# Joints between the stages of a one-layer encoder step: sums moved to VectorE, a kept pool, later norm and bias work, another product order

## The chip, the core and the metric

The kernel runs on one core of a Trainium2 chip. The metric is the device time of one execution in microseconds; the time of a version is the median of its runs. Times inside an execution come from one profiled execution.

## The reference

One inference step of a layer with d_model 2048 over 592 rows (512 prompt frames, 64 sample frames, 16 meta tokens), all in fp32:

```python
h = rmsnorm(x, g_mix)
u, q, k, v = split(h @ w_in)            # 1024 columns each
a = pool_scale * ((trailing_means(u) - u) @ w_pool)      # windows 2, 4, 8, 16
b = (1 - lambda_init) * subln(softmax(q1 k1 + bias) v - lam * softmax(q2 k2 + bias) v)  # 8 heads
x = x + concat(a, b) @ w_out
h = rmsnorm(x, g_ffn)
x = x + (silu(h @ w_gate) * (h @ w_up)) @ w_down         # d_ff 5632
y = rmsnorm(x, g_final)
```

The bias is a relative-position bias, looked up by a one-hot product. The outputs are y and the new rows of the caches and of the pooling state.

## The kernel before

**Precision.** Each fp32 operand is split into a high part (rounded to fp32r, a copy on ScalarE) and a low part (the difference, on VectorE), and each product is three matmuls: high times high, high times low, low times high (`mm3`, L112 to L114; in the class `Seven`, L796 to L798). So every weight tile costs ScalarE one copy and VectorE one subtraction (L137 and L138 with a gain per row, L132 and L133 without, L824 and L825 in the FFN, L994 and L995 in the down projection). Weights are loaded by SyncE's queue into raw tiles, and split from there.

**Order.** The program is written in stages, and a scheduler of the tile framework orders the instructions of each engine by the program's order, by the waits that it knows and by the buffers of the pools. Each engine executes its own list strictly in order; waits between engines are semaphores. What stands in a list behind a waiting instruction waits too.

**Head, to about 54 us.** x is loaded in pieces, transposed on TensorE (L201) and split (L106 on ScalarE, L107 on VectorE) into 16 tiles; `behind` holds the two instructions of the last split. K's first projection runs between the transposes as x and weights arrive; a projection has two halves of the columns, each in a PSUM bank of the pool `pj` (three banks). The rows of the relative-position bias are made by two small matmuls (L243) into two of these banks, copied to `t8` (L244), written to DRAM (`brow`, L247) and from there replicated to 128 partitions in DRAM (`brep`, L248, 3.1 MB), both through GpSimd's queue. Each head loads its piece of it (`bias`, L348) before its scores (L423).

**Heads and pooling projections, to about 583 us.** Eight heads of K, Q, V projections with attention between; then `proj_u(m)` for m = 0 to 7 (evacuation L545). Behind m = 1 come three splits of the attention's outputs (`split_head`), the 16 residual sums of x's high and low part into `hp` (L579, GpSimd), and m = 2 to 7.

**Out-projection, to about 810 us.** `out_proj(m, k0)` for 16 m, first with the second half of the inner dimension while the pooled mean and its map (evacuations L649, L650) run beside, then with the first half (k0 = 0). Between these the weights' pool `wts` is closed and opened anew as `wts2`; the squares of rows 4 to 15 are summed (L692 on ScalarE, L693 on GpSimd) into `accp`. `pre_scale` behind the second of the later out-projections multiplies accp by a matrix of 1/d (L701) for a first estimate of the norm. As the rows are finished, their squares go into `acc` (L755, L757), and `combine` forms the sums of operands that the FFN needs.

**FFN, 810 to 1809 us.** Gate and up are computed by a scheme of seven products per 2x2 block (Strassen and Winograd), for 22 f each. `Seven.prep(i)` makes the weights of product i: 0 is raw "11", 1 a combination of "11", "21" and "22" (L781 to L783), 2 an intermediate, 3 and 5 from "12" and the others (L785), 4 and 6 raw. `product(i)` issues the matmuls, and uses banks 0, 1, 2, 0, 1, 2, 1 for i = 0 to 6, each a running sum; `evac` moves out what stands in the bank before it is used again. `run` issues the products in order and prepares the weights three products ahead. Ahead of the first product `ffn_rstd` multiplies acc (L709) for the exact norm, and three further sets of operands are split (`xput`, L726 and L727).

**Down, 1809 to 2375 us.** 40 blocks (5 rounds x 8 m) of 2 to 5 pairs, 24 of them with 5 pairs, each seven products of 3 matmuls per pair with 288 columns. The operands are loaded from DRAM (`sx`), and split into `hc` (three per pair, for products 0 and 1, 2 and 3, 4 and 5) and `hh` (product 6), L981 and L982. Evacuations of products 1, 2, 4 and 5 are adds on VectorE into y (L1012), the others are copies on ScalarE and accumulating DMAs. The raw weights come into a ring of five buffers (L775), four loads a block. Two memsets (L1022, L1023) and a use of the Sqrt table (L1060) prepare the final norm; the latter is written in a hook behind the first block. The final norm and the output rows follow, to 2397 us.

The parts that the change touches most directly:

```python
for k in range(KT):
    nc.gpsimd.tensor_tensor(hrow(k), xs[k].bitcast(F32)[:, 0, NM:NT], xs[k].bitcast(F32)[:, 1, NM:NT], op=ALU.add)
bank, first = ((0, True), (1, True), (2, True), (0, False), (1, False), (2, False), (1, False))[i]
rw.tile([P, DJ, P], F32, name="raw", tag="raw", bufs=5)
```

Of the kernel before, what the change touches and what calls it, by code (L numbers as in the profile page):

```python
# [19 lines left out]
P = 128  # L20
# [3 lines left out]
NM = 16  # L24
# [26 lines left out]
def hymba_step(  # L51
# [23 lines left out]
    wts_stack = ExitStack()  # L75
# [87 lines left out]
    with tc.tile_pool(name="xraw", bufs=1, side="right") as xp, \  # L163
# [77 lines left out]
        for c0, c1 in ((0, 392), (392, RELW)):  # L241
            ps = pj.tile([P, 512], F32, name="pj")
            nc.tensor.matmul(ps[:HEADS, :c1 - c0], lhsT=tb, rhs=oh[:, c0:c1], start=True, stop=True)  # L243
            nc.vector.tensor_copy(t8[:, c0:c1], ps[:HEADS, :c1 - c0])  # L244
# [333 lines left out]
    for k in range(KT):  # L578
        nc.gpsimd.tensor_tensor(hrow(k), xs[k].bitcast(F32)[:, 0, NM:NT], xs[k].bitcast(F32)[:, 1, NM:NT], op=ALU.add)  # L579
    for m in range(2, HEADS):  # L580
        proj_u(m)
    for h in range(MXB, HEADS):
        split_head(h)
# [81 lines left out]
    wts_stack.close()  # L665
# [9 lines left out]
    wts = ffb.enter_context(tc.tile_pool(name="wts2", bufs=3, reuse_waits="tile"))  # L675
# [10 lines left out]
    for m in range(4, KT):  # L686
        hm = hrow(m)
        if m == 4:
            nc.scalar.activation(accp, hm, AF.Square)
            continue  # L690
        sq = xslot([P, NQ], "sqp")
        nc.scalar.activation(sq, hm, AF.Square)  # L692
        nc.gpsimd.tensor_tensor(accp, accp, sq, op=ALU.add)  # L693
# [67 lines left out]
    class Seven:  # L761


        def __init__(self, src, j0, nj, c0, raws, tmp, splits, xs_, psum, evac):
            self.src = src.rearrange("(j two p) n -> p two j n", p=P, two=2)[:, :, j0:j0 + nj, c0:c0 + 2 * P]
            self.nj, self.raws, self.tmp, self.splits, self.xs_, self.psum, self.evac = nj, raws, tmp, splits, xs_, psum, evac
            self.w, self.a = {}, None
# [21 lines left out]
        def product(self, i):  # L789
            if i == 0:  # L790
                self.b = self.psum()
# [9 lines left out]
    def run(seq, hooks=None, ahead=3):  # L801
        steps = [(n, i) for n in range(len(seq)) for i in range(7)]
        done = 0
        for pos, (n, i) in enumerate(steps):
            while done < len(steps) and done <= pos + ahead:
                dn, di = steps[done]
                seq[dn].load()
                seq[dn].prep(di)
                if di == 2 and dn + 1 < len(seq):
                    seq[dn + 1].load()  # L810
                done += 1
            seq[n].product(i)
            if hooks is not None:
                hooks(n, i)
# [57 lines left out]
    def gate_evac(f):  # L872
        def evac(s, i):
            if i == 0:
# [38 lines left out]
    for i in range(2):  # L913
        seq[0].prep(i)
    ffn_rstd()
    for p, blk in ((3, 2), (5, 3), (6, 1)):
# [4 lines left out]
    prep0 = seq[0].prep  # L921
    seq[0].prep = lambda i: None if i < 2 else prep0(i)
    run(seq)
    ffb.close()
    ffa.close()
    ffr.close()

# [25 lines left out]
    rw.tile([P, DJ, P], F32, name="raw", tag="raw", bufs=5)  # L953
# [11 lines left out]
    def h_free(f, q, n, i):  # L965
# [4 lines left out]
        return k < 0 or (last_use[k // 3], 2 * (k % 3) + 1) <= (n, i)  # L970
# [13 lines left out]
    def hooks(n, i):  # L984
        if queue and h_free(*queue[0], n, i):
            h_operand(*queue.pop(0))
        for f, q in queue:
            assert first_use[f] > n or (first_use[f] == n and 2 * q > i), (f, q, n, i)
# [33 lines left out]
    nc.vector.memset(stat, 1.0)  # L1022
    nc.vector.memset(eps, EPS)  # L1023
# [34 lines left out]
    def finished(n, i):  # L1058
        if n == 0 and i == 6:
# [5 lines left out]
    for n, (m, j0, j1) in enumerate(turns):  # L1065
        psum = (lambda: banks(pz, "mm", "mm")) if n % 2 == 0 else (lambda: banks(pj, "pj", "pj"))
        seq.append(Seven(w_down[0], j0, j1 - j0, m * 2 * P,
                         lambda n, nj=j1 - j0: rw.tile([P, DJ, P], F32, name="raw", tag="raw", bufs=5)[:, :nj],
# [9 lines left out]
    run(seq, hooks)  # L1078
# [60 lines left out]
```

## Time and profile before

| | |
|---|---|
| median of 3 runs | 2395.32 us (2386.61 to 2406.23) |
| the profiled execution | 2398.76 us, span 2396.9 us |
| busy in the span | TensorE 2277.7 us (95%), VectorE 1878.6 (78%), ScalarE 1143.0 (48%), GpSimd 553.7 (23%) |
| matmuls | 16815 |
| chain that ended last | TensorE 79%, DMA 8%, VectorE 7%, ScalarE 2%, GpSimd 1% |
| raw weights of the down projection | 112 loads of 320 KB, 4.5 us from issue to landing |

A busy time is the sum of the instructions' spans on an engine, not the time at its peak: a matmul at the low clock is as busy as one at the high. The chain follows back from the last instruction to what released it, and so shows where the time passed; the list of waits tells what an engine stood idle for, and names the releaser that came last. DMA issues stand as SPq or POOLq, the queues of SyncE and GpSimd.

### The profile page before, as it was taken

How to read it: one execution, taken by the hardware profiler on the slowest of the kernel's cores; microseconds unless marked ns; L12 is line 12 of the kernel's file. 1: busy time of each engine (PE TensorE's matmuls, PEld its weight loads, DVE VectorE, ACT ScalarE, POOL GpSimd, SP SyncE). 2: the span in 40 equal slices, each digit the busy share in tenths (PEclk: the TensorE clock that was granted, in tenths of full speed). 3: DMA queues.
4: the chain of work that ended last, by engine and by line, in shares of the span. 5: the costliest groups of instructions: out<-in, count | busy, mean ns of one | idle time of the engine just before them, and what ended most of it. 6: DMA issues, size and time to landing. Idle time of an engine off the chain costs nothing.

```text
span 2396.9 us, 43624 instructions
## 1 busy us (share of the span) xinstructions
PE 2277.7 (95%) x16815; PEld 2245.9 (94%) x16815; DVE 1878.6 (78%) x3445; ACT 1143.0 (48%) x2423; POOL 553.7 (23%) x483
## 2 busy tenths in 40 slices
PE   7999999979989899999999999999997999999995
PEld 6999999979989899999999999999996999999995
DVE  5888888765557788888888888888886777777786
ACT  5666666633234444444444444444445544444443
POOL 1000000041354322322322322332331022111121
PEclk9999999999989899999999999999998999999998
DMA  7333332223224243333333433433425478766643
GB/s 208 104 88 87 87 97 84 72 62 91 77 65 131 74 132 115 114 124 120 120 116 120 132 108 113 132 114 106 140 89 172 135 184 187 182 158 161 157 101 113
DMA packets 425875, 286.01 MB, mean 119 GB/s; under 512 B 12963, under 2 KB 405341, under 8 KB 425540
## 3 DMA queue, kind: packets, MB, share of 16 engines
q1 hardware_dynamic: 403184, 226.50, 32.9%
q0 software_dynamic: 21648, 55.30, 9.0%
q8 instruction: 132, 2.16, 0.4%
q10 hardware_dynamic: 836, 1.43, 0.2%
q14 instruction: 75, 0.61, 0.1%
HBM read 233.65 MB, written 40.35 MB: 114 GB/s over the span
## 4 chain that ended last, share of the span: by engine, by line
PE 79%; DMA 8%; DVE 7%; issue 3%; ACT 2%; POOL 1%; POOLq 0%; SPq 0%; DVEq 0%; ACTq 0%
PE mm L796 8%; PE pj L796 8%; PE mm L798 8%; PE mm L797 8%; PE pj L798 8%; PE pj L797 8%; PE pj L112 6%; PE pj L113 6%; PE pj L114 6%; DMA raw<-in_w_down_dram 4%; PE mm L114 3%; PE mm L112 3%; PE mm L113 3%; DVE ws L995 2%; DMA sx<-hd 1%
## 5 line engine op out<-in xcount | busy, mean ns | idle before, releaser
L825 DVE TENSOR_TENSOR ws<-raw,ws 128x512 fp32r<-128x512 f32 x430 | 384.5, 910 | 75.0 <-ACT ws L824 72.2
L824 ACT ACTIVATE ws<-raw 128x512 fp32r<-128x512 f32 x430 | 264.5, 630 | 347.5 <-PE pj L798 124.3
L796 PE MATMUL mm<-xc,ws 128*128 128x288 f32 x1232 | 365.4, 297 | 4.5 <-ACT ws L824 4.5
L796 PE MATMUL pj<-xc,ws 128*128 128x288 f32 x1232 | 365.0, 296 | 2.9 <-ACT ws L824 2.9
L797 PE MATMUL pj<-xc,ws 128*128 128x288 f32 x1232 | 363.4, 295 | 0.0
L797 PE MATMUL mm<-xc,ws 128*128 128x288 f32 x1232 | 363.2, 295 | 0.0
L798 PE MATMUL pj<-xc,ws 128*128 128x288 f32 x1232 | 361.9, 294 | 1.0 <-DVE ws L825 1.0
L798 PE MATMUL mm<-xc,ws 128*128 128x288 f32 x1232 | 361.6, 294 | 0.0
L112 PE MATMUL pj<-x,ws 128*128 128x296 f32 (+1 forms) x1024 | 318.3, 312 | 19.2 <-DVE u L545 12.4
L113 PE MATMUL pj<-x,ws 128*128 128x296 f32 (+1 forms) x1024 | 309.0, 302 | 0.0
L114 PE MATMUL pj<-x,ws 128*128 128x296 f32 (+1 forms) x1024 | 306.8, 300 | 0.0
L796 PEld LDWEIGHTS mm<-xc,ws 128*128 128x128 f32 x1232 | 232.0, 188 | 5.9 <-ACT ws L824 5.9
L796 PEld LDWEIGHTS pj<-xc,ws 128*128 128x128 f32 x1232 | 231.9, 188 | 3.1 <-ACT ws L824 3.1
L798 PEld LDWEIGHTS pj<-xc,ws 128*128 128x128 f32 x1232 | 233.3, 189 | 1.5 <-DVE ws L825 1.5
L798 PEld LDWEIGHTS mm<-xc,ws 128*128 128x128 f32 x1232 | 233.3, 189 | 0.0
L797 PEld LDWEIGHTS pj<-xc,ws 128*128 128x128 f32 x1232 | 233.0, 189 | 0.0
L797 PEld LDWEIGHTS mm<-xc,ws 128*128 128x128 f32 x1232 | 233.0, 189 | 0.0
L137 ACT ACTIVATE ws<-wraw,vcols 128x128 fp32r<-128x128 f32 x512 | 169.6, 392 | 126.9 <-PE pj L114 100.6
L112 PEld LDWEIGHTS pj<-x,ws 128*128 128x128 f32 x1024 | 194.3, 190 | 24.0 <-DVE u L545 12.6
L138 DVE SCALAR_TENSOR_TENSOR ws<-wraw,vcols,ws 128x128 fp32r<-128x128 f32 x512 | 169.5, 373 | 45.4 <-ACT ws L137 44.5
L113 PEld LDWEIGHTS pj<-x,ws 128*128 128x128 f32 x1024 | 195.4, 191 | 0.4
L114 PEld LDWEIGHTS pj<-x,ws 128*128 128x128 f32 x1024 | 194.4, 190 | 0.0
(334 smaller groups left out, 5799.9 us busy)
## 6 DMA issues: line engine op xcount, KB each, us to landing
raw<-in_w_up_dram SPq DMA_DIRECT2D x88, 512.0 KB, 3.8
raw<-in_w_gate_dram SPq DMA_DIRECT2D x84, 512.0 KB, 3.7
raw<-in_w_down_dram SPq DMA_DIRECT2D x112, 320.0 KB, 4.5
wraw<-in_w_in_dram SPq DMA_DIRECT2D x64, 512.0 KB, 4.0
hd<-ho POOLq DMA_DIRECT2D x22, 1008.0 KB, 5.4
sx<-hd SPq DMA_DIRECT2D x66, 288.0 KB, 3.2
wraw<-in_w_out_dram SPq DMA_DIRECT2D x32, 512.0 KB, 4.0
y<-ev POOLq DMA_DIRECT2D x60, 144.0 KB, 4.5
```

Of the source, the lines that this page charges most:

```text
L112: nc.tensor.matmul(ps, lhsT=w(0), rhs=x(0), start=first, stop=False)
L113: nc.tensor.matmul(ps, lhsT=w(0), rhs=x(1), start=False, stop=False)
L114: nc.tensor.matmul(ps, lhsT=w(1), rhs=x(0), start=False, stop=last)
L137: nc.scalar.activation(ws[:, 0, k, :], r[:, k, :], AF.Copy, scale=g)
L138: nc.vector.scalar_tensor_tensor(ws[:, 1, k, :], r[:, k, :], g, f[:, 0, k, :], op0=ALU.mult, op1=ALU.subtract)
L796: nc.tensor.matmul(ps, lhsT=w(0), rhs=x(0), start=first and j == 0, stop=False, skip_group_check=True)
L797: nc.tensor.matmul(ps, lhsT=w(0), rhs=x(1), start=False, stop=False, skip_group_check=True)
L798: nc.tensor.matmul(ps, lhsT=w(1), rhs=x(0), start=False, stop=j == self.nj - 1, skip_group_check=True)
L824: nc.scalar.activation(ws[:, 0], src[:, k:k + WK], AF.Copy)
L825: nc.vector.tensor_tensor(ws[:, 1], src[:, k:k + WK], ws.bitcast(F32)[:, 0], op=ALU.subtract)
L995: nc.vector.tensor_tensor(ws[:, 1], src, ws.bitcast(F32)[:, 0], op=ALU.subtract)
```

## The change

Six edits, each at a joint. The copies of the bias rows to `t8` are ordered behind the last split of x. The 16 residual sums move from GpSimd to VectorE, and are written behind the pooling projections m = 2 to 7, two or three each. The pool `wts` stays open to the end of the FFN, `wts2` goes, and the partial squares become a function that is called behind the first of the later out-projections. At the FFN's start the first three products are issued by hand, with `ffn_rstd` behind the second and each set of late splits behind a product; `run` goes on from there. In the down projection the ring of raw weights has six buffers, and the products come in the order 1, 0, 2, 4, 3, 5, 6. The two memsets and the use of the Sqrt table are written behind the fifth block.

```diff
-    wts_stack = ExitStack()
+    wts_stack = ctx.enter_context(ExitStack())
...
-            nc.vector.tensor_copy(t8[:, c0:c1], ps[:HEADS, :c1 - c0])
+            with tc.issue_after(behind[1].ins):
+                nc.vector.tensor_copy(t8[:, c0:c1], ps[:HEADS, :c1 - c0])
...
-    for k in range(KT):
-        nc.gpsimd.tensor_tensor(hrow(k), xs[k].bitcast(F32)[:, 0, NM:NT], xs[k].bitcast(F32)[:, 1, NM:NT], op=ALU.add)
     for m in range(2, HEADS):
         proj_u(m)
+        for k in range(KT * (m - 2) // (HEADS - 2), KT * (m - 1) // (HEADS - 2)):
+            nc.vector.tensor_tensor(hrow(k), xs[k].bitcast(F32)[:, 0, NM:NT], xs[k].bitcast(F32)[:, 1, NM:NT], op=ALU.add)
...
-    wts_stack.close()
...
-    wts = ffb.enter_context(tc.tile_pool(name="wts2", bufs=3, reuse_waits="tile"))
...
-    for m in range(4, KT):
...
+    def partial_squares():
+        for m in range(4, KT):
...
     for m in range(KT):
         out_proj(m, 0)
+        if m == 0:
+            partial_squares()
         if m == 1:
             pre_scale()
...
-    def run(seq, hooks=None, ahead=3):
+    def run(seq, hooks=None, ahead=3, begin=0, done=0, order=range(7)):
...
-        for pos, (n, i) in enumerate(steps):
+        for pos, (n, i) in list(enumerate(steps))[begin:]:
+            step, i = i, order[i]
...
-                seq[dn].prep(di)
+                seq[dn].prep(sorted(order[:2])[di] if di < 2 else order[di])
...
-    for i in range(2):
-        seq[0].prep(i)
-    ffn_rstd()
-    for p, blk in ((3, 2), (5, 3), (6, 1)):
+    seq[0].prep(0)
+    seq[0].prep(1)
+    for k, (p, blk) in enumerate(((3, 2), (5, 3), (6, 1))):
+        seq[0].product(k)
+        seq[0].prep(2 + k)
+        if k == 1:
+            ffn_rstd()
         for j in range(KT // 2):
             xput(p, j, xps[j][:, blk])
...
-    run(seq)
+    seq[1].load()
+    run(seq, begin=3, done=5)
...
+    wts_stack.close()
...
-    rw.tile([P, DJ, P], F32, name="raw", tag="raw", bufs=5)
+    rw.tile([P, DJ, P], F32, name="raw", tag="raw", bufs=6)
...
-    nc.vector.memset(stat, 1.0)
-    nc.vector.memset(eps, EPS)
...
-        if n == 0 and i == 6:
+        if n == 4 and i == 6:
+            nc.vector.memset(stat, 1.0)
+            nc.vector.memset(eps, EPS)
             nc.scalar.activation(stat[:, 0, 15:16], eps, AF.Sqrt)
...
-    run(seq, hooks)
+    run(seq, hooks, order=(1, 0, 2, 4, 3, 5, 6))
```

VectorE's list around the third pooling projection (u_6440 is its result, mx the splits of attention outputs, hp the residual sums). Before:

```order
L500 SCALAR_TENSOR_TENSOR mixb<-mixb,gsub,ny 128x64
L107 TENSOR_TENSOR mx_6449<-mixb,mx_6449 128x576
L107 TENSOR_TENSOR mx_6452<-mixb,mx_6452 128x576
L107 TENSOR_TENSOR mx_6455<-mixb,mx_6455 128x576
L138 SCALAR_TENSOR_TENSOR ws<-wraw,vcols,ws 128x128 x12
L545 TENSOR_TENSOR u_6440<-pj,rstd_bc 128x296
L545 TENSOR_TENSOR u_6440<-pj,rstd_bc 128x232
```

And now, from the third split to the same evacuation:

```order
L107 TENSOR_TENSOR mx_6455<-mixb,mx_6455 128x576
L138 SCALAR_TENSOR_TENSOR ws<-wraw,vcols,ws 128x128 x4
L582 TENSOR_TENSOR hp_6430<-x_191 128x576
L138 SCALAR_TENSOR_TENSOR ws<-wraw,vcols,ws 128x128 x4
L582 TENSOR_TENSOR hp_6430<-x_200 128x576
L582 TENSOR_TENSOR hp_6431<-x_229 128x576
L582 TENSOR_TENSOR hp_6431<-x_238 128x576
L138 SCALAR_TENSOR_TENSOR ws<-wraw,vcols,ws 128x128 x4
L582 TENSOR_TENSOR hp_6432<-x_249 128x576
L582 TENSOR_TENSOR hp_6432<-x_260 128x576
L546 TENSOR_TENSOR u_6440<-pj,rstd_bc 128x296
L546 TENSOR_TENSOR u_6440<-pj,rstd_bc 128x232
```

Two more sums stand ahead of the first split, so that 8 are ahead of this evacuation; the other 8 stand between it and the next.

ScalarE's list at the end of the pooling map (ma its results, hp the rows that are squared, ws the weights of the later out-projections). Before:

```order
L649 ACTIVATE ma_8584<-mm,vcols 128x288 x2
L649 ACTIVATE ma_8603<-mm,vcols 128x288 x2
L689 ACTIVATE accp<-hp_6431 128x576
L692 ACTIVATE sqp<-hp_6431 128x576
L692 ACTIVATE sqp<-hp_6432 128x576 x2
L692 ACTIVATE sqp<-hp_6433 128x576 x2
L692 ACTIVATE sqp<-hp_6434 128x576 x2
L692 ACTIVATE sqp<-hp_6435 128x576 x2
L692 ACTIVATE sqp<-hp_6436 128x576 x2
L132 ACTIVATE ws<-wraw 128x512 x6
```

And now:

```order
L106 ACTIVATE phl<-pp 128x576
L132 ACTIVATE ws<-wraw 128x512 x4
L650 ACTIVATE ma_8584<-mm,vcols 128x288 x2
L650 ACTIVATE ma_8603<-mm,vcols 128x288 x2
L690 ACTIVATE accp<-hp_6431 128x576
L693 ACTIVATE sqp<-hp_6431 128x576
```

Four splits of weights now stand ahead of the map's last evacuations; the squares stand where they stood.

VectorE's list in a full block of the down projection, from the evacuation of product 1 to that of product 5 (y_20611 and y_20602 are the blocks' results). Before:

```order
L1012 TENSOR_TENSOR y_20611<-mm,y_20611 128x288
L995 TENSOR_TENSOR ws<-wt,ws 128x640
L781 TENSOR_TENSOR wt<-raw 128x640
L1012 TENSOR_TENSOR y_20611<-mm,y_20611 128x288
L782 TENSOR_TENSOR raw<-raw 128x640
L995 TENSOR_TENSOR ws<-raw,ws 128x640 x2
L783 TENSOR_TENSOR raw<-wt,raw 128x640
L1012 TENSOR_TENSOR y_20611<-mm,y_20611 128x288
L995 TENSOR_TENSOR ws<-raw,ws 128x640
L1012 TENSOR_TENSOR y_20611<-mm,y_20611 128x288
```

And now:

```order
L1020 TENSOR_TENSOR y_20602<-mm,y_20602 128x288
L1003 TENSOR_TENSOR ws<-raw,ws 128x640
L1003 TENSOR_TENSOR ws<-wt,ws 128x640
L784 TENSOR_TENSOR wt<-raw 128x640
L1020 TENSOR_TENSOR y_20602<-mm,y_20602 128x288
L1003 TENSOR_TENSOR ws<-raw,ws 128x640
L785 TENSOR_TENSOR raw<-raw 128x640
L1020 TENSOR_TENSOR y_20602<-mm,y_20602 128x288
L1003 TENSOR_TENSOR ws<-raw,ws 128x640
L786 TENSOR_TENSOR raw<-wt,raw 128x640
L1003 TENSOR_TENSOR ws<-raw,ws 128x640
L1020 TENSOR_TENSOR y_20602<-mm,y_20602 128x288
```

The third of these evacuations, product 4's, stood behind the third combination (L783) and stands now ahead of it (L786). The memsets and the table load stand in their lists where they stood, behind the last evacuation of the FFN and ahead of the first split of the down projection.

## Rows read from the trace of the kernel before

**Rows 1.** the core's line: span and mean granted TensorE clock.
```profile
core 0: 2396.9 us, clock 0.979
```

**Rows 2.** table by stage: window, us; busy us (x instructions) by engine; clock; DMA share; GB/s.
```profile
487.00:513.00 26.00, 13.63 (x93) 13.40 (x92) 24.64 (x23) 6.84 (x19) 24.10 (x16) 0.82 0.14 41
513.00:583.00 70.00, 70.00 (x514) 70.00 (x513) 32.37 (x91) 27.14 (x75) 2.04 (x3) 0.99 0.32 92
...
696.00:713.00 17.00, 8.23 (x37) 7.88 (x38) 8.82 (x7) 10.05 (x18) 14.61 (x10) 0.60 0.50 131
...
1825.00:2350.00 525.00, 493.68 (x3609) 484.71 (x3607) 406.71 (x642) 261.63 (x506) 92.58 (x99) 0.99 0.64 160
```

**Rows 3.** what TensorE waited for: total us, times, longest us.
```profile
PE pj L112 <- DVE u L545: 12.4, 1, 12.4
PE mm L796 <- ACT hc L981: 10.1, 2, 6.6
PE mm L112 <- ACT ws L132: 8.0, 1, 8.0
PE pj L709 <- POOL acc L757: 6.5, 1, 6.5
...
PE pj L112 <- ACT ws L137: 4.3, 1, 4.3
...
PE mm L114 <- DVE ws L133: 0.9, 1, 0.9
```

**Rows 4.** groups, 1825 to 2350: line, op, tiles xcount | busy, mean ns | idle before, releaser.
```profile
L796 PE MATMUL mm<-hh,ws 128*128 128x288 f32 x86 | 26.5, 308 | 11.5 <-DVE y L1012 11.4
L796 PE MATMUL pj<-hh,ws 128*128 128x288 f32 x83 | 26.4, 318 | 9.6 <-DVE y L1012 9.4
```

**Rows 5.** timeline, 2005.5 to 2009 us: start, us, engine, line, operation.
```profile
2005.56 0.82 DVE L782 TENSOR_TENSOR raw<-raw 128x640 f32<-128x640 f32 x1
...
2007.89 0.45 DVE L1012 TENSOR_TENSOR y<-pj,y 128x288 f32<-128x288 f32 x1
...
2008.49 0.37 PE L796 MATMUL pj<-hh,ws 128*128 128x288 f32 x1 [1.86 <-DVE y L1012]
...
2008.92 0.82 DVE L995 TENSOR_TENSOR ws<-raw,ws 128x640 fp32r<-128x640 f32 x1
```

**Rows 6.** what VectorE waited for, 1825 to 2350 us.
```profile
DVE wt L781 <- DMA raw<-in_w_down_dram: 48.4, 28, 3.2
```

**Rows 7.** groups of instructions as above, all engines, 487 to 512 us.
```profile
L579 POOL TENSOR_TENSOR hp<-x 128x576 f32<-128x576 f32 x16 | 24.1, 1541 | 29.7 <-DVE mixb L500 29.7
L138 DVE SCALAR_TENSOR_TENSOR ws<-wraw,vcols,ws 128x128 fp32r<-128x128 f32 x15 | 18.3, 1283 | 0.0
```

**Rows 8.** timeline, 696.9 to 722 us.
```profile
696.94 6.41 ACT L692 ACTIVATE sqp<-hp 128x576 f32<-128x576 f32 x11
697.69 17.97 POOL L693 TENSOR_TENSOR accp<-accp,sqp 128x576 f32<-128x576 f32 x11 [19.17 <-ACT sqp L692]
...
720.89 1.13 PE L701 MATMUL pj<-accp,ones_d 128*128 128x288 f32 x4
```

**Rows 9.** timeline, two places in the head.
```profile
23.31 0.55 POOL L248 DMA_DIRECT2D brep<-brow  x1 [6.60 <-DMA brow<-t]
...
70.83 0.30 DVE L423 CUSTOM_DVE_ANT_0 e<-S,bias 128x144 f32<-128x144 f32 x1
```

**Rows 10.** DMA issues, 0 to 80 us: out<-in, queue, count, KB each, us to landing.
```profile
brep<-brow POOLq DMA_DIRECT2D x1, 3132.0 KB, 16.7
...
bias<-brep SPq DMA_DIRECT2D x1, 328.0 KB, 4.7
```

**Rows 11.** timeline, 813.5 to 826 us.
```profile
813.50 6.57 POOL L757 TENSOR_TENSOR acc<-acc,sq 128x576 f32<-128x576 f32 x1
...
817.60 1.22 DVE L782 TENSOR_TENSOR wraw<-wraw 128x1024 f32<-128x1024 f32 x1
...
825.69 0.61 PE L796 MATMUL mm<-xc,ws 128*128 128x288 f32 x1 [3.28 <-ACT ws L824]
```

More of the change, by code (lines that the diff above doesn't have):

```diff
@@ L685, in hymba_step @@
     accp = xslot([P, NQ], "accp")
-    for m in range(4, KT):
[L687 to L693, printed above, removed]
+    def partial_squares():
+        for m in range(4, KT):
+            hm = hrow(m)
+            if m == 4:
+                nc.scalar.activation(accp, hm, AF.Square)
+                continue
+            sq = xslot([P, NQ], "sqp")
+            nc.scalar.activation(sq, hm, AF.Square)
+            nc.gpsimd.tensor_tensor(accp, accp, sq, op=ALU.add)
     def halves():
@@ L766, in __init__ @@
             self.nj, self.raws, self.tmp, self.splits, self.xs_, self.psum, self.evac = nj, raws, tmp, splits, xs_, psum, evac
-            self.w, self.a = {}, None
+            self.w, self.a, self.b = {}, None, None
         def load(self):
@@ L789, in product @@
         def product(self, i):
-            if i == 0:
+            if self.b is None:
                 self.b = self.psum()
@@ L799, in product @@
             self.evac(self, i)
-    def run(seq, hooks=None, ahead=3):
+    def run(seq, hooks=None, ahead=3, begin=0, done=0, order=range(7)):
         steps = [(n, i) for n in range(len(seq)) for i in range(7)]
-        done = 0
-        for pos, (n, i) in enumerate(steps):
+        for pos, (n, i) in list(enumerate(steps))[begin:]:
+            step, i = i, order[i]
             while done < len(steps) and done <= pos + ahead:
@@ L813, in run @@
             if hooks is not None:
-                hooks(n, i)
+                hooks(n, step)
     half_no = [0]
@@ L873, in evac @@
         def evac(s, i):
-            if i == 0:
+            if i < 3:
+                return inner(s, i, (None,) * 5, None)
+            if i == 3:
                 gates[f] = fw.tile([P, 2, NQ], F32, name="g")
@@ L920, in hymba_step @@
     fw = ffr.enter_context(tc.tile_pool(name="fw", bufs=1, side="right", reuse_waits="tile"))
-    prep0 = seq[0].prep
-    seq[0].prep = lambda i: None if i < 2 else prep0(i)
-    run(seq)
+    seq[1].load()
+    run(seq, begin=3, done=5)
     ffb.close()
@@ L969, in h_free @@
         k = 3 * f + q - FULL
-        return k < 0 or (last_use[k // 3], 2 * (k % 3) + 1) <= (n, i)
+        return k < 0 or (last_use[k // 3], (1, 4, 5)[k % 3]) <= (n, i)
     def h_operand(f, q):
@@ L987, in hooks @@
         for f, q in queue:
-            assert first_use[f] > n or (first_use[f] == n and 2 * q > i), (f, q, n, i)
+            assert first_use[f] > n or (first_use[f] == n and (0, 2, 3, 6)[q] > i), (f, q, n, i)
         finished(n, i)
@@ L1067, in hymba_step @@
         seq.append(Seven(w_down[0], j0, j1 - j0, m * 2 * P,
-                         lambda n, nj=j1 - j0: rw.tile([P, DJ, P], F32, name="raw", tag="raw", bufs=5)[:, :nj],
+                         lambda n, nj=j1 - j0: rw.tile([P, DJ, P], F32, name="raw", tag="raw", bufs=6)[:, :nj],
                          lambda nj=j1 - j0: rw.tile([P, DJ, P], F32, name="wt", tag="wt", bufs=1)[:, :nj],
```

## The prediction

> **What bounds the kernel now.** I read the cores' line first, then the table by stage, the list of what TensorE waited for, and last the joints one by one. The core ran 2396.9 us at a mean clock of 0.979 [rows 1]; the profiled execution took 2398.8 us, so 1.9 us lie around the span, and it is 3.4 us above the median of the three runs. The sum below is made against 2398.8 and lowered by 3.4 at the end. What a measurement of this kernel can tell from no change is about 1%, 24 us.
>
> The kernel is bound by TensorE wherever it isn't waiting at a joint. A full stretch is 513 to 583 us: 514 matmuls in 70 us, 7.34 per us, or 0.136 us each [rows 2]. Against this, 487 to 513 holds 93 matmuls, 12.7 us of work in 26; and 696 to 713 holds 37, 5.0 us of work in 17, at a granted clock of 0.60, which is a mix of the two levels, 1.2 and 2.4 GHz [rows 2]. So these joints cost 13.3 and 12.0 us. The list of waits says which one ends each: 12.4 us for the evacuation u on VectorE, 8.0 for a weight split on ScalarE, 6.5 for the sum of squares on GpSimd, 4.3 for the third weight chunk of the head, 10.1 (two waits) for the operand splits at the start of the down projection [rows 3]. In the down projection no single wait is large, but it is the largest sum: the first matmul of the product on hh, the seventh and last of each block, waited 11.4 us in one set of banks and 9.4 in the other for VectorE's evacuation y, 20.8 us in all [rows 4].
>
> **Down: order of the products and a sixth raw buffer.** The seventh product accumulates on the bank that the fifth (number 4) left, and must wait until that is evacuated. In the old order only product 5 lies between, 15 matmuls in a full block, 15 x 0.136 = 2.0 us. In one place the trace shows why this isn't enough: VectorE evacuated at 2007.89, behind 2.3 us of queued work that begins at 2005.56, and the product on hh started at 2008.49, 1.86 us late [rows 5]. In the new order (1, 0, 2, 4, 3, 5, 6) two products lie between, 4.0 us, against the 3.5 us that VectorE took there from the end of product 4 (2008.49 - 1.86 - 2.0 = 2004.6) to the end of the evacuation (about 2008.3). The listing shows that this evacuation also moves up in VectorE's queue, ahead of one split and one combination. So nearly all of the 20.8 us can go. Then the weights come next: VectorE already waits 48.4 us in 28 blocks for raw weights, 1.7 each [rows 6], and product 1, which now comes first, needs the set that is prepared second. In the same place that set's last split starts at 2008.92 and ends at 2009.7 [rows 5]; without the late start the block would want its low part at about 2008.49 - 1.86 + 2.0 + 0.3 = 2008.9. So 0.8 us would be missing at such a block, if the raw weights came no earlier. The sixth buffer lets the third load of a block ("22", which the combination needs) take the place that the second combination's source frees, some products before the place it took with five, which shortens the 1.7. Bounds: 26 us (20.8, and 5 more if the raw weights come sooner, a tenth of the 48.4) and 5 us (20.8 less 0.8 in 20 blocks). I take 18, nearer to the row of the hh waits, since that was the wait that ended last.
>
> **Residual sums on VectorE.** On GpSimd the 16 adds took 24.1 us, and beside them 15 weight splits on VectorE took 1.28 us each [rows 7]; VectorE was busy 24.6 of 26 us with 23 instructions, against 32.4 us for 91 in the next 70, 0.36 each [rows 2]. The change takes these 16 adds to VectorE. A difference of two operands in SBUF of 640 columns takes 0.82 there [rows 5], so 576 take about 0.75 (an estimate): 16 x 0.75 = 12.0 us. The listing puts 8 before the evacuation of the third pooling projection and 8 before the fourth. Two projections are 96 matmuls each, 2 x 13.1 = 26.2 us; VectorE's load is 32.4 x 26.2 / 70 = 12.1 us, the adds 12.0 and three splits of that size 2.3: 26.4 us of 26.2. It just fits, so the 13.3 us go but a little of it returns as late weight splits. Bounds: 15 (all, and what the clock gives after) and 6 (VectorE behind by half of the adds). I take 12.
>
> **Weights' pool kept.** The weight splits for the first out-projection stood behind the partial squares, 6.41 us on ScalarE from 696.94 [rows 8]. In the new listing they stand before the last evacuations of the pooling map, so TensorE goes on at 696. But the squares start no earlier, their sums on GpSimd take 18.0 us from 697.69 [rows 8], to 715.7; and the norm's matmul on them stands behind 96 matmuls as before. These end at 696.2 + 12.6 = 708.8, or at 710 where the second group of weight splits runs beside GpSimd; TensorE then waits until 715.7, or until 2 us earlier if the splits beside GpSimd press less. Before, this matmul came at 720.89 [rows 8]: 5.2 to 7.4 us earlier. After so long a wait the clock has to be regained, as it did behind the 8.0: 12.0 - 8.0 - 0.9 = 3.1 us were lost that way [rows 2, 3]. Net 2.1 to 4.3; I take 3.5. Bounds: 0 and 12.
>
> **Head.** Both copies of the bias rows now wait for the last split of x; their two banks of three are held, so only one half of K's projection runs while x arrives. In both listings about 145 matmuls stand before the first transposes of K, 102 of them before the last matmul of x's norm in the old, 56 in the new. The 4.3 us wait for the third weight chunk goes, since ScalarE has x's splits ahead of it. Against it stand 46 more matmuls behind x, 46 x 0.136 = 6.3 us. They are paid out of what x gains: the 4.3, and 46 matmuls fewer in its way, at the low clock in part (an estimate of 4 to 6 us for these). I take a gain of 2. The bias rows: the small write took 6.6 us and the replication 16.7 [rows 9, 10], 23.3 us. From an estimated end of the copies at 42.5, with 0.5 for issuing, this is 66.3, and 4.7 for the load, 71.0 [rows 10]; the scores began at 70.83 [rows 9] and would begin near 69. So some 2 us can return here, but the transfer now runs beside fewer others. Bounds: a loss of 3, a gain of 6.
>
> **Norm and late splits behind the first products.** TensorE's order is the same: 24 matmuls, the norm's two, then product 1. GpSimd's last add (18.0 / 11 = 1.6 us for one of that size [rows 8]) took 6.57 from 813.50 and ended at 820.07, 1.25 after VectorE's last instruction, which began at 817.60 and took 1.22 [rows 11]. The new listing puts one combination (1.22) and three splits of 288 columns (0.45 each, as the evacuation in rows 5) more into VectorE's run, 2.6 us, before its wait for the norm. If the add waits for the end of the run, it comes 2.6 later; the combination is then no longer behind the norm on the way to product 1 at 825.69 [rows 11], which gives back 1.7. If the add isn't held, 1.7 is gained. I take 0, bounds -3 and +3. The Trainium skill (SBUF — State Buffer, section SBUF: two separate sides) says that VectorE operations with two SBUF inputs and GpSimd operations share a pair of ports as an exclusive lock, the later one blocking for the whole instruction. The trace agrees, with the 1.25 us behind VectorE's last instruction; by the rule the joint loses 0.9 us, and the sum would be 2361.
>
> **Memsets and the Sqrt table later.** The listing shows them where they were: the two memsets behind the last FFN evacuation, the table load ahead of the first split of the down projection. ScalarE waits there as before, and the 6.6 us joint (part of the 10.1) stays. 0.
>
> **Sum.** 18 + 12 + 3.5 + 2 + 0 + 0 = 35.5; 2398.8 - 35.5 = 2363.3, less 3.4 for the median: 2360.
>
> **Rivals.** A: the weights set the pace in the down projection. The y waits go, but the raw weights end the wait instead. For it: the 48.4 us, and VectorE's y behind them in the queue; against it: the sixth buffer. Down gives 5 instead of 18: 2373. B: the joints give back. VectorE runs behind in the sums (6), GpSimd's partial sum and the clock eat the out-projection's gain (0), the bias rows the head's (-1): 6 - 1 + 18 = 23, 2372. C: all waits go, at the upper bounds: 26 + 15 + 12 + 6 + 3 = 62, 2333. D, slower: product 1 first makes each block start wait for its second weight set. In the 28 blocks where VectorE waits for raw weights today, a whole product, 2.0 us, would be lost: 56 us, less the 20.8 of the y waits and 17.5 of the other parts: 17.7 slower, 2413. It decides from (20.8 + 17.5) / 28 = 1.4 us per block on; the 0.8 worked out above speaks against it. E: VectorE's longer run holds GpSimd's add at the norm: 2361. F: the change doesn't do what it says; for the memsets this is in the sum.
>
> **Chances.** Forecast 0.40, its own range 2350 to 2371; A 0.22, B 0.12, C 0.10, D 0.07, E 0.09. The range of 2334 to 2388 leaves out half of C and nearly all of D. Faster by over 1%, below 2371.4: the forecast, E, C and not quite half of A and B, 0.70; slower by over 1%, above 2419.3: the far half of D and what I don't see, 0.05; between, 0.25.
>
> **What would show it.** Right: no wait of over 1 us on hh in the down projection; no 12 us gap near 500 and VectorE nearly full there; TensorE at work at 697 and waiting for the partial sum some 5 us near 710; the 6 us joint before the first down product unchanged; K's evacuation a few us before 54. Wrong: raw or ws as the releaser at most block starts (A, D), weight splits late in the third and fourth pooling projection, or scores waiting for the bias load (B).

## The result, and the profile after

The changed kernel took 2366.98 us (median of 6 runs, 2363.18 to 2369.96) against 2393.72 for the kernel before (6 runs, 2385.68 to 2406.23): a ratio of 0.9884, with a 95% interval of 0.985 to 0.9917. That is 26.7 us less, by some 1%; 35.5 were forecast, 2360 inside a range of 2334 to 2388. The profiled executions differ by 28.7 us (spans of 2396.9 and 2368.2), so the stages can be compared one by one. Cut at the first or last start of a line that both kernels have, the spans split like this (us, one profiled execution each):

| stretch | before | after | gained | forecast |
|---|---|---|---|---|
| start to the last scores (VectorE, L423 / L424) | 465.3 | 472.8 | -7.5 | +2 |
| to the last evacuation of u (L545 / L546) | 112.1 | 98.4 | +13.7 | +12 |
| to the norm's estimate on TensorE (L701 / L702) | 143.5 | 138.1 | +5.4 | +3.5 with the next row |
| to the first FFN product | 89.4 | 91.9 | -2.5 | |
| to the first down product | 1005.4 | 1006.4 | -1.0 | 0 |
| to the last evacuation of y (L1012 / L1020) | 559.1 | 538.2 | +20.9 | +18 |
| to the end | 22.1 | 22.4 | -0.3 | 0 |
| sum | 2396.9 | 2368.2 | +28.7 | +35.5 |

So one term is off by its sign: the head. What TensorE waited for in the changed kernel, by the list of waits:

```profile
PE mm L799 <- ACT hc L989: 10.0, 2, 6.6
PE pj L710 <- POOL acc L760: 8.8, 1, 8.8
PE pj L702 <- POOL accp L694: 6.9, 1, 6.9
PE mm L799 <- ACT ws L1002: 6.3, 3, 3.5
...
PE T L376 <- ACT stg L367: 5.2, 1, 5.2
```

Against [rows 3], the wait of 12.4 us for u and the 8.0 for the weights of the out-projection are gone. The 10.1 at the start of the down projection is there as it was (10.0). The sum of squares costs more (8.8 for 6.5), and two waits are new: 6.9 for the partial squares and 5.2 in the head. The table by stage, to hold against [rows 2], shows the two joints (the second window is the old 696 to 713, moved by the 6 us that were gained ahead of it) and the down projection:

```profile
487.00:513.00 26.00, 25.99 (x193) 25.76 (x192) 22.41 (x58) 11.98 (x37) 0.00 (x0) 1.00 0.29 82
...
690.00:707.00 17.00, 12.34 (x94) 12.11 (x93) 8.11 (x9) 10.01 (x18) 14.83 (x10) 1.00 0.22 63
1817.00:2322.00 505.00, 489.50 (x3617) 485.07 (x3617) 415.46 (x644) 267.87 (x505) 92.23 (x99) 0.99 0.68 166
```

193 matmuls where 93 were, at the full clock. GpSimd has nothing there any more, and VectorE is busy 22.4 of 26 us with 58 instructions, not 23. In the down projection the groups on hh, to hold against [rows 4], wait no longer, and VectorE's wait for raw weights, 48.4 us in [rows 6], has nearly gone:

```profile
L799 PE MATMUL mm<-hh,ws 128*128 128x288 f32 x86 | 25.5, 297 | 0.0
...
L799 PE MATMUL pj<-hh,ws 128*128 128x288 f32 x83 | 24.7, 298 | 0.4 <-DVE y L1020 0.4
```

```profile
DVE wt L784 <- DMA raw<-in_w_down_dram: 6.9, 9, 2.8
```

The head, in the timeline of ScalarE, TensorE and VectorE, and in the list of DMA issues for 0 to 80 us (the last column is us from issue to landing):

```profile
63.19 0.63 ACT L399 ACTIVATE vs<-cache 128x512 fp32r<-128x512 f32 x1 [9.39 <-DMA cache<-in_cache_v_dram]
...
65.52 1.12 PE L376 MATMUL T<-ident,cache 128*128 128x128 f32 x4 [5.19 <-ACT stg L367]
...
72.55 0.11 DVE L351 MEMSET bias<- 64x64 f32 x1 [1.15 <-DMA bias<-brep]
...
78.19 0.31 DVE L424 CUSTOM_DVE_ANT_0 e<-S,bias 128x144 f32<-128x144 f32 x1
```

```profile
brep<-brow POOLq DMA_DIRECT2D x1, 3132.0 KB, 14.7
...
cache<-in_cache_v_dram SPq DMA_DIRECT2D x1, 256.0 KB, 14.7
```

The scores begin at 78.19, not at 70.83 [rows 9]. The V cache load of the first head was issued 1.1 us behind the replication of the bias rows, and both took 14.7 us. ScalarE's first use of it (L399) stands in the list ahead of weight splits (L137) and of the copies that free the transposes' banks (L367), so all of these waited 9.4 us, and TensorE behind them 5.2, after which it ran at the low clock (a granted 0.50 from 64 to 68 us). The bias load cost little beside this: VectorE waited 1.15 us for it at 72.55, and TensorE 0.7 us behind that.

### The profile page after: what moved, and what is told of

The parts are those of the page before. It is cut to its first block, busy times and chain, and to the rows that moved or that the text cites. A ratio compares the mean times of both kernels' runs of the same rounds, so it can differ in the third digit from the quotient of the medians.

```text
span 2368.2 us, 43590 instructions
## 1 busy us (share of the span) xinstructions
PE 2274.8 (96%) x16815; PEld 2245.0 (95%) x16815; DVE 1880.0 (79%) x3461; ACT 1150.0 (49%) x2423; POOL 530.3 (22%) x467
## 4 chain that ended last, share of the span: by engine, by line
PE 55%; DVE 4%; DMA 3%; issue 1%; ACT 1%; DVEq 0%; ACTq 0%; SPq 0%
PE pj L799 9%; PE pj L801 9%; PE mm L799 9%; PE pj L800 9%; PE mm L800 9%; PE mm L801 9%; DMA sx<-hd 2%; DVE ws L1003 1%; DMA raw<-in_w_down_dram 1%; DVE y L1020 0%; ACT ws L1002 0%; DVE raw L785 0%; PE mm L1052 0%; DVE ws L828 0%; DVE raw L786 0%
## 5 line engine op out<-in xcount | busy, mean ns | idle before, releaser
L137 ACT ACTIVATE ws<-wraw,vcols 128x128 fp32r<-128x128 f32 x512 | 169.5, 392 | 109.2 <-PE pj L114 88.8
L1002 ACT ACTIVATE ws<-raw 128x640 fp32r<-128x640 f32 (+3 forms) x200 | 133.5, 672 | 126.3 <-DVE raw L786 38.8
```

Source lines behind the costliest of these rows:

```text
L137: nc.scalar.activation(ws[:, 0, k, :], r[:, k, :], AF.Copy, scale=g)
L1002: nc.scalar.activation(ws[:, 0], src, AF.Copy)
```

## Experiments

Each run is the changed kernel with the edit shown. Times are medians; the changed kernel's own is 2366.98. Since the time differs by some us from execution to execution, in the head and in the down projection, the verdicts rest on the stages of the profile as well, one execution each. With six buffers and the new order, VectorE's first to last evacuation y took 526.4 us in the changed kernel, and 518.7 to 529.8 in the ten profiles (its own and nine below) that have its code in this stage. So a difference of a few us there tells nothing by itself, nor does one in the median of four runs.

**The bias rows early again.**

```diff
-            with tc.issue_after(behind[1].ins):
-                nc.vector.tensor_copy(t8[:, c0:c1], ps[:HEADS, :c1 - c0])
+            nc.vector.tensor_copy(t8[:, c0:c1], ps[:HEADS, :c1 - c0])
```

> The changed kernel with one edit undone: the bias rows are copied as soon as they are made. Theory 1: this edit costs 7.5 us, since the replicated rows then travel beside the first V cache load and ScalarE waits 9.4 us for that load. Undone, the wait goes, the last scores start near 465 instead of 472.8, and the time is 2359 (7.5 less). Theory 2: the edit itself gains the 1 us seen at the first transposes of K and the loss comes from elsewhere in the head (the clock after x): then the last scores stay within 2 us of 472 and the time rises by 1.

Measured: 2361.78 (2354.03 to 2371.49, ratio 0.9871, 0.984 to 0.9902). The median is 5 us below the changed kernel, but the intervals overlap, and the runs spread over 17 us where those of the changed kernel spread over 7. The profiled execution is the slowest of the four, and its rows show where it lost. TensorE waited 13.27 us from about 30 us on for x's splits, which stood in ScalarE's list behind a weight chunk that had not landed, while the 3.1 MB travelled (15.7 us from 23.53):

```profile
40.93 2.44 ACT L137 ACTIVATE ws<-wraw,vcols 128x128 fp32r<-128x128 f32 x8 [13.20 <-DMA wraw<-in_w_in_dram]
...
43.97 0.86 PE L112 MATMUL pj<-x,ws 128*128 128x296 f32 x2 [13.27 <-ACT x L106]
```

The wait for the V cache load is gone, as theory 1 had it, but the last scores came at 472.1 in this execution, where theory 1 had 465. For the same chunk the kernel before, early too, waited 2.40 us. That the replication held the chunk up is likely and not shown. The late one always meets the V cache load (a wait of 4.3 to 6.6 us on the same instruction, L376 of the changed kernel, in its profile and in those of the eight runs below with late copies and all of the 3.1 MB sent at once). The last scores came at 470.3 to 475.0 in these nine profiles, and at 465.3 and 472.1 in the two with early copies and one transfer. So the edit made the head slower than the better of the two. That it made it steadier is not shown: the kernel before spread over 7, 11 and 12 us in three other groups of seven runs.

**The replication by heads, first try.**

```diff
-        nc.gpsimd.dma_start(out=rep, in_=row.partition_broadcast(P))
+        nc.gpsimd.dma_start(out=reps[0], in_=row[0].partition_broadcast(P))
...
+            if self.h < HEADS - 1:
+                nc.gpsimd.dma_start(out=reps[self.h + 1], in_=row[self.h + 1].partition_broadcast(P))
```

> The changed kernel with the replication of the bias rows cut into eight parts, one per head: head 0's 0.39 MB where the whole 3.1 MB were, the next head's behind each head's bias load. The copies stay behind x. Theory 1: the 5.2 us TensorE wait near 60 us comes from the 3.1 MB that travel beside the first V cache load; with an eighth of it ScalarE's wait of 9.4 us for that load falls under 2, the last scores start near 465, and the time is 2359 to 2361. Theory 2: the loss lies in the late copies themselves (bank held, bias load late): last scores within 2 us of 472.

Measured: 2366.95 (2362.35 to 2369.74), last scores at 475.0, ScalarE's wait 10.8. This told nothing between the theories: the eight parts have nothing to wait for, and all went out at once, so the same bytes travelled beside the same load.

```profile
48.16 0.55 POOL L249 DMA_DIRECT2D brep<-brow  x1 [1.71 <-DMA brow<-t]
48.70 3.65 POOL L352 DMA_DIRECT2D brep<-brow  x7
```

**The same with early copies.**

> As the run by heads, but with the copies of the bias rows as early as before the change. If the early transfer of 3.1 MB beside x and the weights is what makes the head's time vary from run to run (the kernel before ranges over 20 us, the changed one over 7), an early part of 0.39 MB costs x nothing, K's transposes come at 54 to 57 us, the runs lie within 8 us of each other, and the time is 2357 to 2361, no worse than with late copies. If holding two banks during x is what cost nothing or helped, this is slower than the late copies by 1 to 3.

Measured: 2356.53 (2351.1 to 2359.2, ratio 0.9842, 0.9825 to 0.9858); first scores at 69.0, last at 463.5. The time is below the forecast and clearly below the changed kernel; the reason given was not tested, since here too all parts went out within 4 us. Against the run with early copies and one transfer it is 5 us less, within that run's spread.

**The replication by heads, deferred.** Each later part is tied on GpSimd's queue behind the store of K's rows of the head before.

```diff
+            if self.h < HEADS - 1:
+                with tc.issue_after(stored.ins):
+                    nc.gpsimd.dma_start(out=reps[self.h + 1], in_=row[self.h + 1].partition_broadcast(P))
```

> The changed kernel, late copies kept, with the replication by heads and the parts of heads 1 to 7 really deferred: each is tied on GpSimd's queue behind the store of the head before it (in the first try by heads all eight parts went out within 4 us, so the same 3.1 MB still travelled beside the V cache load). Theory 1 (the bytes beside the V cache load): ScalarE's wait for that load falls from 9.4 to under 2 us, TensorE's 5.2 us wait near 60 us goes, the last scores start near 465 instead of 473 to 475, the time is 2358 to 2361. Theory 2 (the late copies themselves): last scores within 2 us of 472, time within 3 us of 2367.

Measured: 2354.01 (2352.0 to 2359.66, ratio 0.9837, 0.9813 to 0.9862). The wait for the V cache load is gone, the load took 5.3 us, the scores began at 68.4 and ended at 462.8, 10 us earlier than in the changed kernel. The copies were as late as there (the first part went out at 45.29), so it is the bytes that cost, and the late copies themselves little: with early copies and the same deferral (the last run below) the scores ended 3.0 us sooner, one execution each. That is theory 1, and 13 us of the median where 6 to 9 were expected; by the profiles 10 of them are in the head.

```profile
cache<-in_cache_v_dram SPq DMA_DIRECT2D x1, 256.0 KB, 5.3
```

**Five raw buffers, the new order.**

```diff
-    rw.tile([P, DJ, P], F32, name="raw", tag="raw", bufs=6)
+    rw.tile([P, DJ, P], F32, name="raw", tag="raw", bufs=5)
```

> The changed kernel with five raw buffers in the down projection, new order of the products kept. Theory 1: the order alone removes the waits on hh (20.8 us before, 0.0 now), and the sixth buffer only shortens VectorE's wait for raw weights (48.4 before, 6.9 now), which is mostly hidden: hh stays under 2 us, the raw wait returns to some 40, and the time rises by 3 to 6 us. Theory 2: the buffer does most of it, since it is the late raw weights that hold the evacuations up in VectorE's queue: the time rises by 12 or more, with new waits for split weights at the block starts.

**Six raw buffers, the old order.** The bookkeeping of freed operands follows the order.

```diff
-    run(seq, hooks, order=(1, 0, 2, 4, 3, 5, 6))
+    run(seq, hooks)
```

> The changed kernel with the products of the down projection in the old order 0 to 6, six raw buffers kept. Theory 1 (the order): the waits on hh come back at 15 to 21 us, the time rises by 14 to 18. Theory 2 (the buffer): with the raw weights early the evacuation of product 4 is no longer held up, the hh waits stay under 6 us, and the time rises by 5 or less.

Measured: 2381.92 (2379.42 to 2384.08, ratio 0.9953) with five buffers, 2369.48 (2369.02 to 2370.78, ratio 0.9902) with the old order. The stage from VectorE's first to its last evacuation y took 546.7 us before (five, old order), 539.0 with five and the new order, 526.7 with six and the old, 526.4 with both. Theory 2 is right in both runs: the buffer does it. It gives 20.0 us of the stage with the old order (546.7 to 526.7), and with the new one 12.6 (539.0 to 526.4) and 15 of the median; both figures with five buffers lie outside the 518.7 to 529.8 of the ten profiles. With six buffers the order is worth 0.3 us of the stage and 2.5 of the median, which neither the profiles nor the runs (their intervals overlap) tell from nothing; the order's 7.7 with five buffers is the difference of two single executions. VectorE's wait for raw weights with five buffers and with six, each in the down projection:

```profile
DVE wt L784 <- DMA raw<-in_w_down_dram: 45.9, 28, 3.1
```

```profile
DVE wt L784 <- DMA raw<-in_w_down_dram: 8.2, 9, 2.1
```

With six buffers and the old order, the waits on hh sank to 7.2 us by themselves:

```profile
L799 PE MATMUL mm<-hh,ws 128*128 128x288 f32 x86 | 26.7, 311 | 6.6 <-DVE y L1020 6.6
...
L799 PE MATMUL pj<-hh,ws 128*128 128x288 f32 x83 | 24.9, 300 | 0.8 <-DVE y L1020 0.6
```

With five and the new order they were 0.2, but the wait moved to the weights of the block starts:

```profile
PE mm L799 <- ACT ws L1002: 8.6, 6, 4.8
PE pj L799 <- ACT ws L1002: 6.8, 3, 3.4
PE mm L801 <- DVE ws L1003: 2.3, 7, 0.3
...
PE pj L801 <- DVE ws L1003: 2.1, 7, 0.3
```

**The residual sums on GpSimd, written at the new places.**

```diff
-            nc.vector.tensor_tensor(hrow(k), xs[k].bitcast(F32)[:, 0, NM:NT], xs[k].bitcast(F32)[:, 1, NM:NT], op=ALU.add)
+            nc.gpsimd.tensor_tensor(hrow(k), xs[k].bitcast(F32)[:, 0, NM:NT], xs[k].bitcast(F32)[:, 1, NM:NT], op=ALU.add)
```

> The changed kernel with the 16 residual sums on GpSimd again, but written behind the pooling projections m = 2 to 7 as in the change. Theory 1: it is the engine: two-operand instructions of VectorE are held for a whole GpSimd add wherever these stand, so weight splits near 500 to 530 us take over 1 us each, TensorE waits some 8 to 12 us, and the time rises by 8 to 13. Theory 2: it is the place, in one lump ahead of the third projection; spread, they cost 3 us or less.

Measured: 2378.32 (2376.33 to 2380.49, ratio 0.9935): 11.3 us more, and the stretch to the last u 113.3 us instead of 98.4, as before the change. It is the engine. The places alone moved nothing: GpSimd's list holds nothing else there, so the 16 adds ran in one lump as before, and sums really spread over GpSimd's time were not tried. Groups from 490 to 520 us, to hold against [rows 7]:

```profile
L582 POOL TENSOR_TENSOR hp<-x 128x576 f32<-128x576 f32 x16 | 24.1, 1541 | 29.7 <-DVE mixb L501 29.7
L138 DVE SCALAR_TENSOR_TENSOR ws<-wraw,vcols,ws 128x128 fp32r<-128x128 f32 x20 | 19.9, 1049 | 0.1
```

**The norm's estimate one out-projection later.**

```diff
-        if m == 1:
+        if m == 2:
             pre_scale()
```

> The changed kernel with the norm's estimate from the partial squares written one out-projection later. Theory 1: the kept pool let TensorE reach that matmul 6.9 us before GpSimd had summed the squares, and 48 matmuls (6.3 us) between fill that wait; the low clock behind it goes as well: the wait falls under 1.5 us and the time is 6 to 9 us less, 2358 to 2361. Theory 2: what hangs on the estimate (the operands of the FFN) comes later by as much, and the joint at the FFN's start gives it back: 2 us less or none.

Measured: 2360.66 (2357.52 to 2365.11, ratio 0.9862, 0.9839 to 0.9886), 6.3 us less. Theory 1: the wait fell from 6.9 to 1.1 us, and the stretch from the last u to the first FFN product took 221.8 us instead of 230.0 (229.3 to 230.6 in ten other profiles without this edit). Part came back as theory 2 had it: TensorE waited 10.4 us for the last add instead of 8.8.

```profile
707.25 1.24 PE L702 MATMUL pj<-accp,ones_d 128*128 128x288 f32 x4 [1.10 <-POOL accp L694]
...
804.22 2.29 PE L710 MATMUL pj<-acc,ones_d 128*128 128x288 f32 x4 [10.38 <-POOL acc L760]
```

**The start of the FFN as before the change.**

```diff
-    for k, (p, blk) in enumerate(((3, 2), (5, 3), (6, 1))):
-        seq[0].product(k)
...
+    ffn_rstd()
+    for p, blk in ((3, 2), (5, 3), (6, 1)):
...
-    run(seq, begin=3, done=5)
+    run(seq)
```

> The changed kernel with the start of the FFN as it was before (the norm ahead of the first product in the program, late splits in one lump). Theory 1: the edit put 2.6 us more into VectorE's run that holds GpSimd's add off; undone, the add takes 6.6 us again instead of 8.8, TensorE waits 6.5 for it, and the second product still waits 3.3 us for its weights behind the norm instead of 1.4: both nearly cancel, the time is within 2 us. Theory 2: the edit gained by the late splits spread behind the products: undone, 3 us more or above.

Measured: 2366.19 (2363.81 to 2372.09, ratio 0.9892, 0.9863 to 0.9921): within 1 us, theory 1. The changed kernel at this place, GpSimd's add, VectorE's last split, the norm's matmul and product 1, and then the same with the edit undone:

```profile
804.37 8.80 POOL L760 TENSOR_TENSOR acc<-acc,sq 128x576 f32<-128x576 f32 x1
...
811.46 0.46 DVE L728 TENSOR_TENSOR xc<-xlast,xc 128x288 fp32r<-128x288 f32 x1
...
813.22 2.29 PE L710 MATMUL pj<-acc,ones_d 128*128 128x288 f32 x4 [8.76 <-POOL acc L760]
...
816.95 0.61 PE L799 MATMUL mm<-xc,ws 128*128 128x288 f32 x1 [1.44 <-ACT ws L827]
```

```profile
804.11 6.56 POOL L760 TENSOR_TENSOR acc<-acc,sq 128x576 f32<-128x576 f32 x1
...
808.21 1.21 DVE L785 TENSOR_TENSOR wraw<-wraw 128x1024 f32<-128x1024 f32 x1
...
810.73 2.29 PE L710 MATMUL pj<-acc,ones_d 128*128 128x288 f32 x4 [6.33 <-POOL acc L760]
816.29 0.61 PE L799 MATMUL mm<-xc,ws 128*128 128x288 f32 x1 [3.28 <-ACT ws L827]
```

The add ends 1.25 us behind VectorE's last instruction in both (813.17 against 811.92, and 810.67 against 809.42), as in [rows 11]. The longer run costs 2.4 us (8.76 less 6.33), the earlier weights give 1.8 back (3.28 less 1.44).

**The last add on VectorE.**

```diff
-            nc.gpsimd.tensor_tensor(acc, acc, sq, op=ALU.add)
+            (nc.vector if m == KT - 1 else nc.gpsimd).tensor_tensor(acc, acc, sq, op=ALU.add)
```

> The changed kernel with the last add of the sum of squares on VectorE instead of GpSimd. Theory 1: that add takes 8.8 us on GpSimd because VectorE's run of two-operand instructions holds it off to the run's end; on VectorE it takes 0.75, TensorE's wait for it falls from 8.8 to under 3 us, and some of the time at the low clock behind it goes too: 6 to 9 us less, 2358 to 2361. Theory 2: the split weights for the second product are the next wait at the same place (they came 1.4 us behind the norm) and give most of it back: 2 us less.

Measured: 2361.51 (2359.81 to 2363.59, ratio 0.9859, 0.9845 to 0.9874), 5.5 us less, between the two theories. The wait for the sum fell from 8.8 to 0.7, and the weights of product 1 became the next wait, 6.1 us. From the norm's estimate to the first down product it took 1092.2 us instead of 1098.3 (1096.9 to 1098.1 in seven other profiles with the changed kernel's code there):

```profile
804.59 1.24 PE L710 MATMUL pj<-acc,ones_d 128*128 128x288 f32 x4 [0.71 <-DVE acc L760]
811.98 0.61 PE L799 MATMUL mm<-xc,ws 128*128 128x288 f32 x1 [6.15 <-ACT ws L827]
```

**Memsets and table load really later.**

```diff
+            with tc.issue_after(marks["dve"].ins), tc.issue_after(marks["act"].ins):
                 nc.vector.memset(stat, 1.0)
                 nc.vector.memset(eps, EPS)
                 nc.scalar.activation(stat[:, 0, 15:16], eps, AF.Sqrt)
```

> The changed kernel with the two memsets and the use of the Sqrt table tied behind a weight split of the fifth block, so that they do stand later in their lists. Theory 1: the table's wait for the memset behind the FFN's last evacuation holds ScalarE's first splits of the down projection for 11 us; moved, these run under the last FFN products, TensorE's waits of 6.6 and 3.5 us at the joint fall to under 4 in all, and the time is 6 to 9 us less, 2358 to 2361. Theory 2: VectorE's list puts its part (combinations and low parts) behind the last evacuations anyway, and the joint keeps 6 of its 10 us: 3 us less.

Measured: 2362.12 (2361.58 to 2367.66, ratio 0.9867, 0.985 to 0.9883). The median is 5 us lower, and the rows don't show why: in the profiled execution, the slowest of the four, the head was 1.9 us ahead by the last scores, and the joint itself gained nothing, 5.4 and 5.3 us instead of 6.6 and 3.5, 10.7 in all. ScalarE's first split ran 12 us sooner, but the second waits for VectorE's combinations behind the last evacuations, and the second pair's operands for their loads. At the joint this is theory 2, and less than it gave.

```profile
1804.58 0.85 PE L799 MATMUL mm<-hc,ws 128*128 128x288 f32 x2 [5.36 <-ACT hc L989]
1812.74 0.85 PE L799 MATMUL mm<-hc,ws 128*128 128x288 f32 x2 [5.32 <-ACT hc L989]
```

**The parts that helped, together.** Early copies of the bias rows, the deferred replication, the last add on VectorE, the estimate one out-projection later.

> The change without its first edit (bias copies early again) and with three of its joints mended: the replication by heads, deferred as above; the last add of the squares on VectorE; the norm's estimate one out-projection later. If the parts add up (9 us from early copies by heads, 6 from the add, 6 to 8 from the estimate), 2343 to 2347. If the joints share one slack, the estimate's gain coming back as a longer wait at the FFN's start, 2350 to 2354.

Measured: 2339.71 (2337.52 to 2342.45, ratio 0.9774, 0.9752 to 0.9796): 27 us below the changed kernel and 55 below the one before that ran beside it. The medians of the deferral, the add and the estimate alone give 13.0, 5.5 and 6.3, 24.8 in all, so the parts add up, and the time is 3 us below the lower of the two forecasts. Its last scores came at 459.8, and the stretch from the last u to the first FFN product took 222.1 us. What TensorE waited for most:

```profile
PE mm L801 <- ACT hc L991: 10.0, 2, 6.6
PE mm L801 <- ACT ws L1004: 7.3, 3, 4.4
PE mm L801 <- ACT ws L829: 6.3, 2, 6.1
```

## Why the prediction was right, and where not

**The whole.** The time lies in the range, 7 us above the forecast. By terms, three of the four that were to gain did (20.9, 13.7, 2.9 for 18, 12, 3.5), and the two taken as 0 came out as -1.0 together. The head was to gain 2 and lost 7.5, which is 9.5 us; the other stretches gave 2.7 more than forecast, which leaves the sum 6.8 short (28.7 for 35.5). Two sums of the working are slips that move no term: from 2004.6 to 2008.3 is 3.7 us, not 3.5, and the norm's estimate comes 5.2 to 7.2 us earlier, not 7.4.

**Down: the size held by luck, the reason did not.** The step that failed is to take the "2.3 us of queued work that begins at 2005.56" as what made the evacuation late, which the new order would cover since "two products lie between". That work was late for a cause of its own, a few rows ahead of the ones that were read:

```profile
2003.05 0.82 DVE L781 TENSOR_TENSOR wt<-raw 128x640 f32<-128x640 f32 x1 [2.78 <-DMA raw<-in_w_down_dram]
```

VectorE had stood 2.8 us for a raw weight block, more than the 1.86 by which the product on hh was late, and from there to the evacuation it worked without a pause. The wait on hh named VectorE, and the root was the ring of five buffers. Both readings were in the text, the 20.8 us at TensorE and the 48.4 at VectorE, but taken as two separate things, of which the second was to limit the first; the buffer was given 5 us at most, in the upper bound. The runs with one edit each show that the buffer alone gives 20.0 of the 20.3 us of the stage. The order alone, with five buffers, gives 7.7; the size came out because both edits were in the one change. With five buffers rival A happened as told, the wait on hh gone and one on split weights in its place. Rival D, a whole product lost at the block starts, did not happen in any run.

**Residual sums: right.** 8 and 8 adds in two projections, 0.76 us each, VectorE busy 22.4 of 26 us, not quite as full as worked out, and TensorE not waiting; the change of engine is what did it.

**Weights' pool: right, with the wait that was foretold.** TensorE worked on where it had waited 8.0 us and then waited 6.9 for the partial sum, where the text gave 5.7 to 6.9 (from 708.8 or 710 to 715.7), or up to 2 less. The stretch to the estimate took 5.4 us less, and the next one 2.5 more; behind the wait the granted clock was 0.50 from 708 to 712 and 0.72 from 712 to 716. This rests on the two profiles: no run undoes this edit alone.

**Norm: right in both directions.** 2.4 us lost to the longer run, 1.8 regained, for 2.6 and 1.7 worked out; the rival E, by which GpSimd's add is held to the end of VectorE's run, is what happened. The Trainium skill (SBUF — State Buffer, section SBUF: two separate sides) says that VectorE's operations with two SBUF inputs and GpSimd's share a pair of ports as an exclusive lock, held for the whole instruction. The rows agree in that one engine held the other off, and go further: the add was held for a whole run of VectorE's instructions, 8.80 us where one of its size took 1.40 at 713.38.

**Memsets: right that they did not move.** That moving them would have brought nothing at the joint was not known; the run shows it for one execution.

**Head: wrong.** The failed step is "the transfer now runs beside fewer others", with the bias load as the only thing that could be late. The transfer did take 14.7 us instead of 16.7 and landed at 62.1 us, before the 66.3 of the working, and the bias load held VectorE up by only 1.15 us. K's evacuation came 3.4 us earlier (50.58 for 53.96) and its first transposes 1.1 (56.4 for 57.5), so x's part of the term gained; what was lost came behind them. What was left out is who else loads in that time: SyncE's queue has the first head's K and V cache loads right behind the weights (51.8 to 55.2 us before, 47.5 to 49.9 now), and the replication, moved from 23 to 47 us, met them. The first scores were put near 69 and began at 78.19. With seven eighths of the transfer out of the way they began at 68.4.

## What to carry to other kernels

Follow a late instruction back through its engine's own list, until the wait that made the whole list late; the releaser that a wait names may itself have stood behind a load, and then a buffer can do more than an order, as it did here. When a transfer is moved, list every load that is issued while it will travel, on all queues, and what stands in the lists behind their first users. A GpSimd add that is short alone was held here for the whole of a run of VectorE's: on VectorE it took the wait for it from 8.8 us to 0.7, though the next wait gave part of that back. Measure how much a stage varies with the same code before pricing an edit by one profile of it.

## What was not expected of the hardware

A 256 KB load beside a 3.1 MB transfer took 14.7 us, as long as the large one, against 5.3 beside an eighth of it. In 0 to 80 us the queue of the large transfer moved 3.93 MB in 768 packets, 5.1 KB each, and SyncE's moved 10.30 MB in 13908, 0.74 KB each. The Trainium skill (DMA: Bandwidth & Descriptors, section Queues, rings and completion order) says that each DMA engine goes round the queues packet by packet. That would give the queue with small packets the smaller share, and agrees with the two landings; that this is the cause, no run here shows.

With early copies of the bias rows and one transfer, the head differs much between two executions: TensorE waited 13.27 us for x near 30 us in one, and in the other, the profile of before, 2.5 for x and 4.3 for a weight split. Why the chunk came so late in the one, no run here shows. In the down projection the same code took 518.7 to 529.8 us in ten executions, and what varies there is open too.
